# The second layer's mixer: input projection as seven half products, retention and mixing behind it

## The chip, the cores and the metric

One core of a Trainium2 chip. The metric is the device time of one execution in microseconds (us), the median of several runs; profiles show one execution, by engine: TensorE (PE, its weight loads PEld), VectorE (DVE), ScalarE (ACT), GpSimd (POOL) and SyncE's queue (SP), which issues every DMA here.

## The reference

Two layers over 1024 rows of width 1024, f32. Each layer computes x <- LN(alpha x + mixer(x)) and then x <- LN(alpha x + SwiGLU(x)), with 2816 hidden columns. The change concerns the mixer of layer 1 (the second):

```
hproj = x @ w_in_odd            # 1024 x 2560: q 256, k 256, v 512, gate 512, z-part 1024 (u 512, z 512)
o_c = group_norm_heads(retention(q, k, v)) * silu(gate)         # 4 heads
u, z = gelu(...);  z = layer_norm(z);  o_d = u * (tril(w_s) @ z + b_s)   # blocks of 128 rows, 4 groups
mix = concat([o_c, o_d]) @ w_out_odd
```

## The kernel before

Every f32 product is three passes of f32r matmuls (high x high, high x low, low x high). So each operand is split into a high and a low part: an ACT cast and a DVE subtraction (`split`, L64 to L67). Weights come from HBM through raw tiles (3 to 4) into weight units of 128 x 2 x 512 (a ring of 8, with more of them in the feed-forward stages).

Activations stand transposed in X tiles (128 features x 4 blocks of features x high, low x 512 rows). `row_to_x` (L144) makes 128 rows of one: four PE transposes into a PSUM bank, an ACT cast, and for the low part either a DVE subtraction or (pe=True) another matmul and ACT cast; then the bank is free.

The feed-forward stages (`rest`, L852) already use seven half products for a 2 x 2 block product (Winograd's form, in place of eight): the weights of a column pair are combined on DVE (`others`), seven operands are split and seven products of 12 matmuls run into PSUM banks, with sums between. The down product loops over half products i = 1, 5, 6, 3, 7, 2, 4; behind them come the row norms, and `transposed` makes X tiles for the next layer: the second half of the rows first for each block, the two transposing banks being taken in program order.

`odd_mixer` (L627) projects without that: `gemm_T` (L113) with 512 moving columns for q, k, gate and u (`proj_T`), `gemm_R` (L123) with 256 for v and z, 24 matmuls per output block over all 8 feature blocks. `gate()` makes z first, block of rows by block of rows. Then `weave` fills the gaps of retention's chains (scores, values, group norm, output) with projection steps: a main generator yields its cost, and so much of the fill times a rate is issued behind it. PE's order in the mixer is this written order (manual_schedule); the other engines are ordered by Tile's list scheduler, by priority and a simulated time.

`OutProj` (L193) takes finished 128-row pieces of the transposed mixer output (`take`: stored to o_rows in HBM, the last kept), reads them back and splits them (`split_o`), and multiplies in two halves of the contraction: `first` (pieces 0 to 3, retention's, 16 products of 12 matmuls with ALPHA x added) and `second` (pieces 4 to 7). `first` asks for the first rows of the other half itself if the kept piece is there; `middle` reads the rest.

## Time and profile before

| what | value |
|---|---|
| median of 3 runs | 2304.25 us (2302.89 to 2306.63) |
| profiled execution | 2303.7 us, span 2302.0 us, mean granted clock 0.995 |
| busy share of the span | PE 98%, PEld 82%, DVE 66%, ACT 40%, POOL 5% |
| the chain that ended last | PE 82%, DVE 8%, DMA 6%, ACT 2% |
| HBM | 218.64 MB read, 87.56 MB written |

The second layer's mixer runs from about 1256 us (first z matmul) to 1588 us (end of the first half of its output projection). PE records are pipelined and overlap: a group's mean is longer than the spacing of its matmuls, which is read from the chain (a stretch's time over its count).

### The profile page before, as it was taken

How to read it: one execution, taken by the hardware profiler on the slowest of the kernel's cores; microseconds unless marked ns; L12 is line 12 of the kernel's file. 1: busy time of each engine (PE TensorE's matmuls, PEld its weight loads, DVE VectorE, ACT ScalarE, POOL GpSimd, SP SyncE). 2: the span in 40 equal slices, each digit the busy share in tenths (PEclk: the TensorE clock that was granted, in tenths of full speed). 3: DMA queues.
4: the chain of work that ended last, by engine and by line, in shares of the span. 5: the costliest groups of instructions: out<-in, count | busy, mean ns of one | idle time of the engine just before them, and what ended most of it. 6: DMA issues, size and time to landing. Idle time of an engine off the chain costs nothing.

```text
span 2302.0 us, 30422 instructions
## 1 busy us (share of the span) xinstructions
PE 2258.9 (98%) x11380; PEld 1878.4 (82%) x11380; DVE 1512.4 (66%) x3030; ACT 918.0 (40%) x1756; POOL 124.5 (5%) x111
## 2 busy tenths in 40 slices
PE   8999999999999999999999999999999999999997
PEld 7888888878788888888887988888788888888885
DVE  4767676777877676756577423455967776656568
ACT  4545455553543333334443321122543333334432
POOL 0000000001200000000021100000300000000003
PEclk9999999999999999999999999999999999999998
DMA  5212121234255454558655111144345454558553
GB/s 170 69 47 59 42 58 37 67 98 132 79 178 188 147 169 141 174 194 290 200 184 180 47 47 42 47 130 158 126 140 169 147 182 134 178 182 294 187 179 136
DMA packets 195539, 312.37 MB, mean 136 GB/s; under 512 B 14784, under 2 KB 98368, under 8 KB 195392
## 3 DMA queue, kind: packets, MB, share of 16 engines
q1 hardware_dynamic: 195392, 310.44, 41.3%
q8 instruction: 89, 1.46, 0.2%
q14 instruction: 58, 0.48, 0.1%
HBM read 218.64 MB, written 87.56 MB: 133 GB/s over the span
## 4 chain that ended last, share of the span: by engine, by line
PE 82%; DVE 8%; DMA 6%; ACT 2%; issue 1%; POOL 0%; POOLq 0%; SPq 0%; ACTq 0%; DVEq 0%
PE pd L1110 9%; PE bx_g L875 8%; PE bx_u L875 8%; PE bw_u L875 5%; PE bw_g L875 5%; PE vps L127 4%; PE qps L117 4%; PE kps L117 3%; PE po_o L234 3%; PE bv_u L875 3%; PE bv_g L875 3%; PE bz_u L875 2%; PE bz_g L875 2%; DMA raw_d<-d_ops 2%; PE ovps L127 2%; PE zps L127 2%
## 5 line engine op out<-in xcount | busy, mean ns | idle before, releaser
L1110 PE MATMUL pd<-w_d,h 128*128 128x512 f32 x1716 | 393.3, 390 | 3.5 <-DVE w_d L67 2.1
L1110 PEld LDWEIGHTS pd<-w_d,h 128*128 128x128 f32 x1716 | 322.0, 188 | 72.8 <-DVE w_d L67 3.5
L875 PE MATMUL bx_g<-xs,w_g 128*128 128x512 f32 x792 | 192.2, 390 | 0.5 <-ACT w_g L66 0.5
L875 PE MATMUL bx_u<-xs,w_u 128*128 128x512 f32 x792 | 190.9, 389 | 0.0
L875 PEld LDWEIGHTS bx_g<-xs,w_g 128*128 128x128 f32 x792 | 148.2, 188 | 32.2 <-ACT w_g L66 0.8
L875 PEld LDWEIGHTS bx_u<-xs,w_u 128*128 128x128 f32 x792 | 148.6, 188 | 30.8
L67 DVE TENSOR_TENSOR w_d<-raw_d,w_d 128x512 fp32r<-128x512 f32 x149 | 97.7, 686 | 103.1 <-ACT w_d L66 102.9
L66 ACT CAST w_d<-raw_d 128x512 fp32r<-128x512 f32 x149 | 86.6, 618 | 152.9 <-DMA raw_d<-d_ops 88.9
L875 PE MATMUL bw_u<-xs,w_u 128*128 128x512 f32 x528 | 130.7, 389 | 0.0
L875 PE MATMUL bw_g<-xs,w_g 128*128 128x512 f32 x528 | 130.7, 389 | 0.0
L67 DVE TENSOR_TENSOR h<-raw_h,h 128x512 fp32r<-128x512 f32 x143 | 98.8, 715 | 33.4 <-ACT h L66 33.0
L440 ACT ACTIVATE s<-s,mx 128x640 f32<-128x640 f32 (+7 forms) x128 | 93.3, 731 | 65.6 <-DVE mx L438 65.3
L875 PEld LDWEIGHTS bw_u<-xs,w_u 128*128 128x128 f32 x528 | 99.0, 188 | 21.0 <-DVE cy L926 0.4
L127 PE MATMUL vps<-w_v,x 128*128 128x256 f32 x768 | 114.5, 293 | 1.5 <-DVE k L340 1.5
L875 PEld LDWEIGHTS bw_g<-xs,w_g 128*128 128x128 f32 x528 | 99.0, 188 | 20.5
L117 PE MATMUL qps<-x,w_q 128*128 128x512 f32 x384 | 110.0, 408 | 0.6 <-ACT w_q L66 0.5
L117 PE MATMUL kps<-x,w_k 128*128 128x512 f32 x384 | 110.5, 408 | 0.0
L66 ACT CAST h<-raw_h 128x512 fp32r<-128x512 f32 x143 | 83.8, 618 | 59.1 <-DMA raw_h<-h_ops 52.2
L127 PEld LDWEIGHTS vps<-w_v,x 128*128 128x128 f32 x768 | 100.8, 193 | 6.5 <-issue 4.6
L66 ACT CAST w_u<-raw_u 128x512 fp32r<-128x512 f32 x118 | 73.3, 623 | 77.8 <-issue 40.9
L67 DVE TENSOR_TENSOR w_u<-raw_u,w_u 128x512 fp32r<-128x512 f32 x118 | 80.8, 686 | 35.5 <-ACT w_u L66 35.4
L66 ACT CAST w_g<-raw_g 128x512 fp32r<-128x512 f32 x110 | 68.3, 625 | 88.2 <-PE bw_g L875 30.8
(591 smaller groups left out, 4184.9 us busy)
## 6 DMA issues: line engine op xcount, KB each, us to landing
raw_h<-h_ops SPq DMA_DIRECT2D x70, 512.0 KB, 4.2
h_ops<-cy SPq DMA_DIRECT2D x110, 256.0 KB, 3.3
raw_g<-in_ffn_w_gate_dram SPq DMA_DIRECT2D x44, 512.0 KB, 4.7
raw_u<-in_ffn_w_up_dram SPq DMA_DIRECT2D x44, 512.0 KB, 5.4
raw_dr<-in_ffn_w_down_dram SPq DMA_DIRECT2D x44, 512.0 KB, 3.6
d_ops<-raw_dr SPq DMA_DIRECT2D x44, 512.0 KB, 2.7
raw_d<-d_ops SPq DMA_DIRECT2D x40, 512.0 KB, 4.9
raw_d<-in_ffn_w_down_dram SPq DMA_DIRECT2D x30, 512.0 KB, 4.8
```

What stands on the lines that cost most here:

```text
L66: A.copy(dst[:, 0], src)
L67: V.tensor_sub(dst[:, 1], src, dst[:, 0].bitcast(F32))
L117: T.matmul(ps, w[k // 4][:, a, (k % 4) * P:(k % 4 + 1) * P], xh[k // 4][:, k % 4, b, :], start=n == 0, stop=n == 3 * KT - 1)
L127: T.matmul(ps, xh[k // 4][:, k % 4, a, b4 * P:(b4 + 1) * P], ws[k // 2][:, b, (k % 2) * 256:(k % 2) * 256 + 256], start=n == 0, stop=n == ...
L234: T.matmul(ps, self.xo[h][c][:, k, a, b4 * P:(b4 + 1) * P], self.w[c][2 * nh + k // 2][k % 2][:, b], start=n == 0, stop=n == 11)
L440: A.activation(s[:, :L], s[:, :L], AF.Exp, bias=self.mx[:, m:m + 1], scale=0.125, accum_out=self.sm[:, m:m + 1])
L875: T.matmul(ps, w[:, a, k * P:(k + 1) * P], X[i][:, k, b, :], start=first and n == 0, stop=n == 11, skip_group_check=more or not first)
L1110: T.matmul(bank[side][b4], hs[k][:, a, b4 * P:(b4 + 1) * P], ds[k][:, b], start=fresh and k == 0 and n == 0, stop=k == NP - 1 and n == 2, ...
```

## The change

The layer's input projection is done as seven half products over 512 x 512 blocks of x. v and z together are one such block product (`rows_product`: seven of 48 matmuls, 512 moving columns, k outside and the four row blocks inside). q, k, u and gate are six column pairs (`pair`: seven products of 12 matmuls). The combined weights for v and z are made in the first layer's gate and up loop (`row_ops`, rounds 0 to 3) and stored in z_ops. X1, X2, X3 and X7 come from the end of the first layer; X6, X4 and X5 from sums of the rows in place (`sums`), transposed between the products. u and gate go to HBM (gu_rows) and are read back; u, then gate, into one tile. Only then come retention and mixing: mixing woven into head pair 0's states, then both pairs' heads woven with `first`, whose half is now the mixing's (begin=4). y tiles, misc, qk and gu share one pool of two.

```diff
-        def __init__(self, dram, res, name):
+        def __init__(self, dram, res, name, begin=0):
...
         def take(self, k, h, o):
+            k = (k - self.begin) % KT
...
+    def row_weights(i, pick=None):
+        c, h = {1: (512, 0), 2: (512, 1), 4: (2048, 1)}.get(i, (0, 0))
+        r = []
+        for j in (0, 2):
+            if i in (1, 2, 4):
+                src = w_in_odd[0][(4 * h + j) * P:(4 * h + j + 2) * P, c:c + 512].rearrange("(k p) f -> p k f", p=P)
+            else:
+                src = z_ops[i in (3, 5), j:j + 2, :, slice(0, 512) if i in (6, 3) else slice(512, 1024)].rearrange("k p f -> p k f")
+            r += load_w(src, f"zw{i}_{j}", pick)
+        return r
...
+        op = OutProj(w_out_odd[0], res, "o", begin=4)
...
+                def rows_product(ps, i, ds, first=True):
+                    for k in range(4):
+                        for b4 in range(4):
+                            for n, (a, b) in enumerate(PASSES):
+                                T.matmul(ps[b4], X[i][:, k, a, b4 * P:(b4 + 1) * P], ds[k][:, b], start=first and k == 0 and n == 0,
+                                         stop=k == 3 and n == 2, skip_group_check=True)
+                def sums():
+                    for b4 in range(4):
+                        y0a, y0b, y1a, y1b = (y[h][:, b4, c * 512:(c + 1) * 512] for h in (0, 1) for c in (0, 1))
+                        V.tensor_sub(y1a, y1a, y0a)
+                        V.tensor_sub(y1b, y1b, y1a)
+                        V.tensor_sub(y0b, y1b, y0b)
+                    for i, h, c in ((6, 1, 1), (4, 0, 1), (5, 1, 0)):
+                        for b4 in range(4):
+                            row_to_x(y[h][:, b4, c * 512:(c + 1) * 512], X[i], b4, trp, f"o{i}{b4}")
+                z = banks(False, "p3")
+                rows_product(z, 3, zw)
...
+                f = banks(True, "p7")
+                rows_product(f, 7, row_weights(7))
...
+                rows_product(z, 1, row_weights(1))
...
+                sums()
+                f = banks(True, "p2")
+                rows_product(f, 2, row_weights(2))
...
+                rows_product(z, 6, row_weights(6), first=False)
...
+                rows_product(f, 4, row_weights(4))
+                misc = ypool.tile([P, 4, 1024], F32, tag="y", name="misc")
...
+                for b4 in range(4):
+                    V.tensor_sub(zv[:, b4], zv[:, b4], f[b4])
+                    z_rows(b4)
+                rows_product(z, 5, row_weights(5), first=False)
+                for b4 in range(4):
+                    V.tensor_add(v[:, 4 + b4], z[b4], v[:, 4 + b4])
+                    V.tensor_add(zv[:, 4 + b4], z[b4], zv[:, 4 + b4])
+                    z_rows(4 + b4)
...
+                qk = ypool.tile([P, 4, 1024], F32, tag="y", name="oqk")
+                pair(256, qk[:, 2:4], "ok")
+                pair(0, qk[:, 0:2], "oq")
+                for n, (c0, func) in enumerate(((1536, AF.Gelu_apprx_tanh), (1792, AF.Gelu_apprx_tanh),
+                                                (1024, AF.Silu), (1280, AF.Silu))):
+                    c = pair(c0, misc[:, 0:2], f"gu{n}")
+                    for i in (0, 3, 2, 1):
+                        A.activation(c[i], c[i], func)
+                        S.dma_start(gu_rows[n][:, i // 2, (i % 2) * 512:(i % 2 + 1) * 512], c[i])
...
+            gu = ypool.tile([P, 4, 1024], F32, tag="y", name="gu")
+            for n in (0, 1):
+                S.dma_start(gu[:, 2 * n:2 * n + 2], gu_rows[n])
...
+            def mixing():
+                yield from ws_transposed()
+                for g in range(4):
+                    yield from mixed(g)
+                for n in (0, 1):
+                    S.dma_start(gu[:, 2 * n:2 * n + 2], gu_rows[2 + n])
             r0, r1 = Retention(0), Retention(1)
-            weave([], [gate()], 0)
-            weave([ws_transposed()], [r0.qkv()], 1.0)
-            weave([r0.heads()], [r0.gates(), r1.qkv()], 3.6)
-            weave([r1.heads()], [r1.gates(), mix(0), mix(1)], 2.4)
             first = op.first()
-            for g in range(4):
-                weave([mixed(g)], [mix(g + 2)] if g < 2 else [first] if g == 3 else [], 5.0)
+            weave([r0.states()], [mixing()], 3.0)
+            weave([r0.heads()], [first], 1.3, rest=False)
+            weave([r1.states(), r1.heads()], [first], 1.7)
             op.middle()
...
+            def row_ops(j):
+                r = [raw_tile(f"zr_{j}_{i}") for i in (0, 1)]
+                for i in (0, 1):
+                    for z, c in ((0, 512), (1, 2048)):
+                        S.dma_start(r[i][:, z * 512:(z + 1) * 512], w_in_odd[0][(4 * i + j) * P:(4 * i + j + 1) * P, c:c + 512])
...
+                        if not last and p < 4:
+                            row_ops(p)
...
+                    if h:
+                        row_to_x(yb, xn[3], b4, trp, nm + "c", pe=True)
+                        t3 = raw_tile(f"t3_{nm}")[:, :512]
+                        G.tensor_sub(t3, yb, ya)
+                        row_to_x(t3, xn[7], b4, trp, nm + "g", pe=True)
+                    else:
+                        row_to_x(ya, xn[1], b4, trp, nm + "a")
+                        row_to_x(yb, xn[2], b4, trp, nm + "b")
```

## Rows read from the trace of the kernel before

**Rows 1.** Busy time by stage: window, length, PE, PEld, DVE, ACT, POOL, clock, DMA.

```profile
640.00:1033.00 393.00, 393.00 (x1735) 325.05 (x1733) 273.28 (x433) 147.71 (x259) 0.00 (x0) 1.00 0.51 170
1257.00:1310.00 53.00, 51.35 (x420) 50.10 (x419) 26.76 (x52) 22.24 (x47) 7.64 (x8) 1.00 0.24 68
...
1356.00:1447.00 91.00, 91.00 (x519) 77.09 (x518) 34.18 (x97) 15.84 (x30) 4.05 (x4) 1.00 0.15 47
```

**Rows 2.** The chain of waits, 1180 to 1700: start, length in us, engine, tile, line.

```profile
1275.04 35.76 PE zps L127 x298
1310.80 0.44 PE wsps L663 x4
1311.23 10.92 PE oq0ps L117 x48
...
1370.35 1.08 PE rs L750 x8
...
1515.39 0.89 PE mix L813 x8
...
1654.86 2.73 PE bx_u L875 x12
```

**Rows 3.** Busy time of the z product alone at the entry (PE, PEld, ACT).

```profile
1256.10:1269.00 12.90, 9.27 (x66) 8.45 (x67) 0.73 (x2) 1.00 0.68 189
```

**Rows 4.** Timeline at the entry: start, length, engine, line, operation.

```profile
1268.16 0.60 PE L148 MATMUL xt_f<-ident,yf 128*128 128x128 f32 x4
...
1268.80 0.59 ACT L151 CAST xn<-xt_f 128x512 fp32r<-128x512 f32 x1 [1.29 <-PE xt_f L148]
1269.42 0.69 DVE L156 TENSOR_TENSOR xn<-xt_f,xn 128x512 fp32r<-128x512 f32 x1 [1.18 <-ACT xn L151]
...
1271.87 1.08 ACT L154 CAST xn<-xt_f 128x512 fp32r<-128x512 f32 x2
```

**Rows 5.** Groups by line, 1033 to 1350: the norm of z on DVE.

```profile
L182 DVE SCALAR_TENSOR_TENSOR zv<-zv,rstd_sgu,gb_sgu 128x512 f32<-128x512 f32 x8 | 6.0, 751 | 3.1 <-POOL rstd_sgu L169 3.1
L181 DVE SCALAR_TENSOR_TENSOR zv<-zv,mv_sgu,gb_sgu 128x512 f32<-128x512 f32 x8 | 5.9, 743 | 0.0
L164 DVE BATCH_NORM_STATS2 st_sgu<-zv 128x6 f32<-128x512 f32 x8 | 5.5, 693 | 1.7 <-ACT zv L677 1.7
```

**Rows 6.** DMA issues of the whole run: count, KB each, median us to landing.

```profile
raw_h<-h_ops SPq DMA_DIRECT2D x70, 512.0 KB, 4.2
h_ops<-cy SPq DMA_DIRECT2D x110, 256.0 KB, 3.3
...
raw_h<-h_ops SPq DMA_DIRECT2D x14, 256.0 KB, 3.7
...
o_rows_o<-oTr SPq DMA_DIRECT2D x8, 256.0 KB, 2.0
...
o_rows_o<-oTm SPq DMA_DIRECT2D x6, 256.0 KB, 4.1
```

**Rows 7.** Groups by line, 1355 to 1600: ACT and DVE operations of mixing and output.

```profile
L66 ACT CAST xo_o<-raw_o_o 128x1024 fp32r<-128x1024 f32 x6 | 6.3, 1050 | 21.0 <-PE po_o L234 10.2 <-DMA raw_o_o<-o_rows_o 8.2 <-PE u3ps L117 2.6
...
L815 DVE TENSOR_TENSOR mixs<-mix,bsb 128x512 f32<-128x512 f32 x8 | 5.4, 687 | 9.9 <-PE mix L813 9.9
...
L717 ACT ACTIVATE og<-og00ps 128x512 f32<-128x512 f32 x2 | 1.2, 599 | 9.8 <-PE og00ps L117 9.8
```

**Rows 8.** The chain of waits, 1352 to 1372: one state update of retention.

```profile
1359.72 0.43 PE kv L735 x2
```

**Rows 9.** Timeline at the end of the first half of the output projection.

```profile
1549.07 47.26 PE L234 MATMUL po_o<-w_o,xo_o 128*128 128x512 f32 x207
...
1588.22 0.37 SPq L88 DMA_DIRECT2D raw_o_o<-o_rows_o  x1
...
1592.92 1.57 ACT L66 CAST xo_o<-raw_o_o 128x1024 fp32r<-128x1024 f32 x2 [3.52 <-DMA raw_o_o<-o_rows_o]
```

**Rows 10.** Busy time in the burst of row norms at the end of the run.

```profile
2260.00:2270.00 10.00, 4.29 (x15) 2.61 (x14) 10.00 (x7) 0.70 (x2) 6.59 (x3) 0.81 0.39 141
2270.00:2280.00 10.00, 10.00 (x39) 8.06 (x39) 9.45 (x21) 0.00 (x0) 1.46 (x1) 0.85 0.11 44
```

More of the change, by code (lines that the diff above doesn't have):

```diff
@@ L273, in second, with product, kf, operand @@
                 yield 0.65
+    def product(ps, w, x, first=True, more=False):
+        n = 0
+        for k in range(4):
+            for a, b in PASSES:
+                T.matmul(ps, w[:, a, k * P:(k + 1) * P], x[:, k, b, :], start=first and n == 0,
+                         stop=n == 11, skip_group_check=more or not first)
+                n += 1
+    def kf(t):
+        return t.rearrange("p (k f) -> p k f", k=4)
+    def operand(src, i, nm):
+        u = w_unit(f"{nm}_{i}")
+        split(u.rearrange("p z (k f) -> p z k f", k=4), src)
+        return u
+    def row_weights(i, pick=None):
[8 more added lines that the diff above has]
+        return r
     def even_mixer():
@@ L649, in odd_mixer @@
[L649 removed]
+            bsb = p1.tile([P, 4, P], F32, name="bsb")
             S.dma_start(bsb, sgu_b[0].partition_broadcast(P))
@@ L790, in heads @@
                     self.sT, self.orow = {}, {}
-                    yield from self.states()
                     self.oT = [op_.tile([P, SEQ], F32, tag="oT", name=f"oTr_{self.p}{z}") for z in (0, 1)]
@@ L802, in heads @@
                             yield 1.0
-            def mix(g):
-                uT = uTs[g] = p2.tile([P, SEQ], F32, tag="uT", name=f"uT_{g}")
-                yield from proj_T(1536 + g * P, f"u{g}", lambda ps, sl: A.activation(uT[:, sl], ps, AF.Gelu_apprx_tanh))
             def mixed(g):
@@ L868, in rest @@
             X = [None] * 8
-            def product(ps, w, i, first=True, more=False):
-                n = 0
-                for k in range(4):
-                    for a, b in PASSES:
-                        T.matmul(ps, w[:, a, k * P:(k + 1) * P], X[i][:, k, b, :], start=first and n == 0,
-                                 stop=n == 11, skip_group_check=more or not first)
-                        n += 1
-            def kf(t):
-                return t.rearrange("p (k f) -> p k f", k=4)
-            def operand(src, i, nm):
-                u = w_unit(f"{nm}_{i}")
-                split(u.rearrange("p z (k f) -> p z k f", k=4), src)
-                return u
             def start(dram, p, nm):
@@ L894, in first_two @@
                 bx = accp.tile([P, 512], F32, tag="acc", name=f"bx_{nm}")
-                product(bx, m[2], 1, more=True)
+                product(bx, m[2], X[1], more=True)
                 bz = mm_tile(f"bz_{nm}")
-                product(bz, m[3], 2)
+                product(bz, m[3], X[2])
                 return bx, bz
@@ L1040, in transposed @@
                 def transposed(h, b4):
-                    for c in (0, 1) if not last else ():
-                        row_to_x(y[h][:, b4, c * 512:(c + 1) * 512], xn[h][c], b4, trp, f"f{layer}{h}{b4}{c}", pe=h == 1)
+                    if last:
+                        return
+                    ya, yb = y[h][:, b4, ca], y[h][:, b4, cb]
+                    nm = f"f{layer}{h}{b4}"
+                    if h:
[6 more added lines that the diff above has]
+                        row_to_x(yb, xn[2], b4, trp, nm + "b")
                 def sum_up(i, b4, ps):
```

177 lines of the change are left out of this document (104 added, 73 removed).

## The prediction, made before the change was run

> **What bounds the kernel now.** I read the page's shares first: TensorE (PE) is busy 98% of the span, so only work taken off it, or waits put on it, can move the end. Then the stages [rows 1]: the first layer's gate and up stage, and the second layer's projections with retention show PE busy for their whole length; the entry to the second layer loses 1.65 us of 53. DVE is at 70% in the gate and up stage and at 38% in the retention stage, with room. Then the chain of waits, for the real price of a matmul: the records overlap, so I take a stretch of the chain and divide by its count. A moving operand of 512 columns costs 10.92/48 = 0.2275 us in the old projections and 2.73/12 = 0.2275 in a seven-product stage; 256 columns cost 35.76/298 = 0.120 [rows 2].
>
> **Matmuls removed and added.** Before, query, key, gate and u take 12 column blocks x 48 = 576 matmuls of 512 columns, 131.0 us; value and z take 2 x 384 = 768 of 256 columns, 92.2 us; together 223.2. After, six pairs of 84 and seven row products of 48 make 840 of 512 columns: 191.1. Twelve more groups of four transposes, for X6, X4 and X5, take 0.44 each [rows 2], 5.3. PE's own work falls by 223.2 - 191.1 - 5.3 = **26.8 us**.
>
> The Trainium skill, page "TensorE: Matmul & The Clock Gate", section "Back-to-back issue gap", gives N/2.4 GHz + 2.5 ns between issues at full clock: 0.216 us for 512 and 0.109 for 256 columns, which would save 576 x 0.216 + 768 x 0.109 - 840 x 0.216 = 26.7 us before the transposes, not 32.1, and the sum below would end 5.4 us later. Here the trace differs, most for the narrow ones (0.120), and I keep the rows.
>
> Everything else is about what PE waits for.
>
> **Entry.** The old first projection went row block by row block and needed only the finished block; it did 66 matmuls between 1256.1 and 1269 [rows 3], while the last blocks were still being transposed. The new p3 goes over k outside and all four blocks inside, so it stands until the last block of X3 is in. That block comes late because the transposes take turns in two PSUM banks in program order: one bank is held from the transposes (1268.16) over the ACT cast (1268.80) to the end of the DVE subtraction (1269.42 + 0.69), and the last block of the second half has its low part only at 1271.87 + 1.08 [rows 4]. Without ACT's copies and its table load for the old product I put X3 at 1269. Until then p3 can issue 9 matmuls, 2.0 us, where the old one had 66 x 0.12 = 7.9: **+6** (4 if the banks turn faster, 7.5 at 1272).
>
> **The sums.** PE's order here is written by hand: p1, then all 12 transpose groups, then p2. Two banks, 1.95 us each from transposes to release and some 0.15 to the next start [rows 4]: 6 x 2.1 = 12.6 us, of which 5.3 is work counted above: **+7.3**. If only DVE set the pace, 12 x 0.69 + 1.3 less 5.3 = 4.3; with four weight splits of p6 (0.69 each) between them, 10. The subtractions on y before them lie under p7 and p1 (22 us).
>
> **Row norms.** Behind p4 and p5 DVE gets 12 evacuations of 0.69 and eight row norms, each statistics 0.69 and two passes of about 0.75 [rows 5], 25.8 us in all, while PE has p5 (10.9) and two pair products (5.5) before it needs operand 6, for which DVE must also make three combinations and a split (2.8). 28.6 - 16.4 = 12, less what was done ahead in the 2 us before p4's end and what finds gaps while a norm waits for POOL's power: **+3**, from 0 to 9. Six pairs follow, each with 19.1 us on PE and some 10.5 on DVE; the gate and up stage runs the same mix with no PE wait [rows 1], so no charge.
>
> **The last phase.** E is the end of the last pair. The misc tile holds that pair's results, and the gu tile takes its slot, so the reload of u waits for: addition 0.69, Silu 0.6, store of 256 KB 3.3, read of 1 MB. For that size there is no row; 512 KB takes 4.2 and 256 KB 3.7 [rows 6], so 5.2 by their step, 8.4 as two reads in line. I take 5.2, as the queue is quiet there. u is there at E + 9.8. The Trainium skill, page "DMA: Bandwidth & Descriptors", section "Bandwidth", has 6.15 us for 1 MB, which would add 1 us to the sum.
> DVE then goes through 12 operations of 0.69 (bias and product of each mixing half) to the first half of the last group: E + 18.1. The row is stored (between 2.0 and 4.1, I take 3.0), read back (4.2) and cast (1.05) [rows 6, 7]: the third block of the first output product can run at E + 26.3. By the hand-written order PE has until there: states 2 x 0.44 + 7 x 0.43, transposing the mixing weights 0.44, eight mixing halves of 0.89, two score groups of 1.08 and six output matmuls [rows 2, 8]: 3.9 + 0.4 + 7.1 + 2.2 + 1.4 = 15.0. **+11.3.** All of head 0's values, later scores and output stand behind this product on PE. Low end, the shortest rows everywhere (both stores 2.0, the big read 4.2): 8; high end, the double read, 14 state updates and four weight splits between, a 4.1 store: 23. The constant tables (decay, mask, biases) are loaded at E - 2.7, when X5's memory comes free; SP issues them ahead of the gu reads, and they land under this wait. The gates' own reload follows the mixing and has over 20 us.
>
> **The tail.** Walking the weave's costs by hand, the place in the first half of the output projection that asks for the first rows of its other half now passes before head 3's first half is taken; so both reads of retention rows fall behind the first half, where before only one did. Before, the first half ended at 1549.07 + 171 x 0.2275 = 1588.0 (192 matmuls, 21 of them earlier), such a read was issued at 1588.22 and cast from 1592.92 [rows 9]; the next product then waited for nothing, as its half had been there. After, it waits for that cast, 1592.92 + 1.05 - 1588 = 6, less two transposes of 0.44: **+5** (0 if the read is issued earlier, 8 with the second cast).
>
> **First layer.** Four times in the gate and up stage come four reads of 256 KB, four DVE operations (2.7 us in a round of 38) and two stores; the cover is DVE's 30% and the lookahead of the raw tiles: **+0.5** (0 to 3). Four POOL subtractions at its end lie under the last product. Twenty-four more SP issues of some 0.35 us are spread over 150 us.
>
> **Clock.** Where PE was busy 4.3 of 10 us, the granted clock was 0.81 on the mean, and 0.85 in the next 10 us with PE full [rows 10], a mean of the full level (2.4 GHz) and the lower one (1.2): 1.5 us lost after one such wait. The last phase has one of that kind, the entry and the sums milder ones: **+2.5** (0 to 6).
>
> **Sum:** -26.8 + 6 + 7.3 + 3 + 11.3 + 5 + 0.5 + 2.5 = +8.8. The profiled execution took 2303.7 (span 2302.0 and 1.7 around it), 0.55 under the median of the runs, so nothing is shifted: **2312 us**. All low ends together give -26.8 + 16.3 = -10.5, all high ends some +40.
>
> **Rivals.**
> Forecast, 0.42: the waits as summed, 2303 to 2324.
> Last phase not held, 0.32: the mixing rows are back before PE needs them, because the list scheduler puts reload, mixing and store ahead of all else on SP and DVE. It decides from the point where the third output block can run at E + 15 in place of E + 26. Then 11.3 and 1.5 of clock go: 2299, between 2288 and 2306. For it: DMA moves only 47 to 68 GB/s in the old retention stage and DVE is a third busy. Against it: the chain store, read, 12 operations, store, read is serial whatever the order.
> DVE becomes the bound behind p4, 0.16: with strict program priority operand 6 waits for all eight norms, some 9 us more, and the last phase lies at its upper half: 2324, up to 2335. For it: DVE full and PE at 4.3 of 10 in a burst of norms [rows 10]; against it: those rows are twice as wide.
> The saving is smaller than counted, 0.10: the new products run above their 0.2275 for want of operands, since the pairs have 8 weight units and 3 raw tiles where the gate and up stage has 12 and 4. A quarter of the 26.8 missing gives 2319. Against it: PE there needs one operand in 2.7 us, and ACT and DVE make one in 0.7.
>
> **Numbers.** 0.2% (4.6 us) is about what can be told from no change. Faster: 0.03 + 0.18 + 0 + 0.01 = 0.22; within: 0.05 + 0.12 + 0 + 0.03 = 0.20; slower: 0.58. The range runs from the better part of the second case to most of the third, 2291 to 2332; the forecast's own range is 2303 to 2324.
>
> **What would show it.** Entry: PE with few p3 matmuls and a wait for ACT on X3. Sums: 48 transposes spread over about 12 us. Row norms: a PE wait for DVE on the first key pair's sixth operand. Last phase: some 11 us in which PE waits for the cast of the output's first operand, behind a read of gu rows. Tail: a PE wait of 5 us behind the read of retention rows. The prediction is wrong if the last phase shows PE full, or if the stage from p3 to the last pair is longer than about 76 + 115 + 5 + 17 us.

## The result, and the profile after

The changed kernel takes 2337.69 us (median of 4, 2334.34 to 2339.92) against 2303.57 (2301.43 to 2306.63) for the kernel before: ratio 1.0152, 95% interval 1.014 to 1.0164, so 34 us slower. Slower was forecast, but at 2312 and no more than 2332. The page of the changed kernel, with its span, PE's busy time and the granted clock:

```profile
span 2337.4 us, 29811 instructions
...
PE 2255.4 (96%) x10924; PEld 1851.0 (79%) x10924; DVE 1597.2 (68%) x3168; ACT 943.5 (40%) x1790; POOL 131.2 (6%) x115
...
PEclk9999999999999999999999999989999999999999
```

PE has 456 matmuls fewer than before (11380), yet its busy time fell by 3.5 us only, and it stands idle for 82 us in place of 43. Its mean clock went from 0.995 to 0.986. So of the 35.4 us between the two spans 39 are idle time, and the matmuls, which had 26.8 us less to do, took some 23 us longer than counted. An estimate from the mean clocks puts most of that down to the lower clock: (1 - clock) x span is 32.7 us after and 11.5 before.

**Where the time is lost.** The lag of the new kernel behind the old at marks that both traces have:

| mark | before | after | lag |
|---|---|---|---|
| first down product, layer 0 | 1033.90 | 1039.97 | 6.1 |
| first matmul of the second mixer | 1256.18 | 1268.57 | 12.4 |
| end of the output projection's first half | 1588.0 | 1622.5 | 34.5 |
| first down product, layer 1 | 2072.62 | 2116.64 | 44.0 |
| end of the span | 2302.0 | 2337.4 | 35.4 |

Stages of the changed kernel (columns as in [rows 1]); the first row answers to the first of [rows 1], where PE was busy throughout:

```profile
640.00:1033.00 393.00, 387.75 (x1707) 319.73 (x1706) 278.14 (x443) 140.23 (x249) 0.00 (x0) 1.00 0.56 187
...
1320.00:1340.00 20.00, 19.19 (x79) 15.57 (x80) 8.73 (x14) 5.31 (x10) 0.00 (x0) 0.83 0.17 54
1360.00:1380.00 20.00, 17.39 (x71) 13.94 (x70) 20.00 (x41) 7.56 (x13) 4.70 (x4) 0.91 0.17 53
...
1500.00:1520.00 20.00, 17.21 (x96) 14.78 (x96) 14.12 (x30) 1.63 (x2) 0.64 (x1) 0.79 0.64 231
1520.00:1540.00 20.00, 10.91 (x34) 7.47 (x34) 7.78 (x10) 3.13 (x3) 0.00 (x0) 0.64 0.76 266
1540.00:1560.00 20.00, 20.00 (x92) 15.21 (x92) 10.63 (x39) 0.00 (x0) 2.03 (x2) 0.93 0.13 42
1620.00:1640.00 20.00, 13.09 (x47) 9.42 (x46) 16.49 (x34) 6.34 (x9) 1.01 (x1) 0.87 0.74 235
```

What PE waited for from 1265 to 1700 us (us in total, times, longest):

```profile
PE po_o L237 <- ACT xo_o L66: 11.5, 3, 8.0
PE wsps L815 <- POOL wsr L808: 5.3, 1, 5.3
PE xt_o L148 <- DVE xn L156: 4.5, 5, 1.6
PE po_o L237 <- DVE ym L275: 3.7, 1, 3.7
PE bw_gu L284 <- DVE misc L768: 3.1, 4, 0.8
PE bx_ok L284 <- DVE zv L739: 2.6, 1, 2.6
```

Each is a place of its own: last phase and tail, last phase, sums, tail, pairs, norms. The sums and a pair on PE, as timeline:

```profile
1311.50 1.03 PE L148 MATMUL xt_o<-ident,yf 128*128 128x128 f32 x8
1314.18 1.25 PE L148 MATMUL xt_o<-ident,yf 128*128 128x128 f32 x8 [1.65 <-DVE xn L156]
...
1324.24 6.13 PE L687 MATMUL p<-w_zw,xn 128*128 128x512 f32 x19
...
1407.61 2.88 PE L284 MATMUL bw_oq<-xn,w_oq 128*128 128x512 f32 x12
1411.27 3.06 PE L284 MATMUL bw_oq<-xn,w_oq 128*128 128x512 f32 x12 [0.78 <-DVE oqk L768]
```

The transposes go two by two as the banks come free and take 1324.24 - 1311.50 = 12.7 us with 5.3 of work in them. In a pair the seventh product adds to the bank that the sixth has just filled; DVE must read it first (L768), and as PE's order is written by hand nothing else stands between: 0.78 us, six times over. The last phase on PE, then the same stretch on SP's queue:

```profile
1494.79 0.60 PE L841 MATMUL krps<-ident,oqk 128*128 128x128 f32 x4
1500.73 1.12 PE L815 MATMUL wsps<-ident,wsr 128*128 128x128 f32 x4 [5.34 <-POOL wsr L808]
...
1531.33 3.34 PE L237 MATMUL po_o<-w_o,xo_o 128*128 128x512 f32 x6 [8.03 <-ACT xo_o L66]
```

```profile
1514.33 0.42 SPq L951 DMA_DIRECT2D gu<-gu_rows  x1
1515.15 7.99 SPq L207 DMA_DIRECT2D o_rows_o<-oTm  x4
1523.18 0.43 SPq L951 DMA_DIRECT2D gu<-gu_rows  x1
1523.72 1.79 SPq L88 DMA_DIRECT2D raw_o_o<-o_rows_o  x3
```

With E = 1494.8 the end of the last pair, the third output block runs at E + 36.5, in place of the E + 26.3 of the forecast. And behind the first half, the tail:

```profile
1622.49 1.84 PE L896 MATMUL rt<-ident,orow 128*128 128x128 f32 x8
1627.53 7.40 PE L237 MATMUL po_o<-w_o,xo_o 128*128 128x512 f32 x24 [3.20 <-ACT xo_o L66]
1638.59 12.57 PE L237 MATMUL po_o<-w_o,xo_o 128*128 128x512 f32 x48 [3.65 <-DVE ym L275]
```

24 matmuls of 512 columns took 7.40 us here, 0.31 each in place of 0.2275. In the first layer the profile has PE waits that were not there before, and one of DVE (640 to 1045, DVE to 800):

```profile
PE bw_g L284 <- DVE cy L1020: 3.9, 2, 3.0
PE bw_u L284 <- DVE cy L1020: 1.3, 1, 1.3
```

```profile
DVE zr L1043 <- DMA zr<-in_w_in_odd_dram: 14.8, 4, 5.4
```

DVE stands 3.7 us a round, and runs nothing meanwhile, in front of row_ops' first combination, whose reads have not landed. The additions of the products (cy, L1020), for which PE waits, stand behind it in DVE's queue.

### The profile page after: what moved, and what is told of

Its sections match the earlier page's. It is cut to its first block, busy times and chain, and to the rows that moved or that the text cites. A ratio compares the mean times of both kernels' runs of the same rounds, so it can differ in the third digit from the quotient of the medians.

```text
span 2337.4 us, 29811 instructions
## 1 busy us (share of the span) xinstructions
PE 2255.4 (96%) x10924; PEld 1851.0 (79%) x10924; DVE 1597.2 (68%) x3168; ACT 943.5 (40%) x1790; POOL 131.2 (6%) x115
## 4 chain that ended last, share of the span: by engine, by line
PE 82%; DVE 10%; DMA 4%; ACT 2%; issue 2%; POOL 0%; SPq 0%; POOLq 0%; DVEq 0%; ACTq 0%
PE pd L1231 16%; PE bx_u L284 7%; PE bx_g L284 7%; PE bw_g L284 4%; PE bw_u L284 4%; PE vps L127 4%; PE qps L117 4%; PE po_o L237 4%; PE kps L117 3%; PE p L687 3%; PE bv_u L284 2%; PE bz_g L284 2%; PE bz_u L284 2%; PE bv_g L284 2%; PE po_e L237 2%; PE pv L521 2%
## 5 line engine op out<-in xcount | busy, mean ns | idle before, releaser
L237 PE MATMUL po_o<-w_o,xo_o 128*128 128x512 f32 x384 | 106.0, 420 | 16.6 <-ACT xo_o L66 11.5
L237 PEld LDWEIGHTS po_o<-w_o,xo_o 128*128 128x128 f32 x384 | 73.2, 198 | 35.0 <-ACT xo_o L66 12.1
```

Source lines behind the costliest of these rows:

```text
L237: T.matmul(ps, self.xo[h][c][:, k, a, b4 * P:(b4 + 1) * P], self.w[c][2 * nh + k // 2][k % 2][:, b], start=n == 0, stop=n == 11)
```

## The experiments

Marks of single profiled executions scatter by some 2 us, and medians of four runs by about as much (the single runs of one version lie up to 18 us apart), so segments between two marks of one trace are read beside the times. The versions were timed in groups, each beside the kernel before, which took 2302.2 to 2305.0 in them; a ratio is to the kernel before in the same group. "The pairs" is from the first key product to E, "behind E" from E to the first down product of layer 1 (621.9 us in the changed kernel).

**row_ops on POOL, and without row_ops.** In row_ops the four `V.tensor_...` become `G.tensor_...`:

```diff
-                V.tensor_add(wb1, wb0, wb1)
+                G.tensor_add(wb1, wb0, wb1)
```

> The four combinations of each round of row_ops run on POOL instead of DVE; loads and stores stay as they are. Theory (queue order): in the changed kernel DVE stands 14.8 us in four rounds in front of these combinations, waiting for its own reads (3.7 us a round), and the first layer's products wait for DVE behind it. POOL has nothing to do in that stage, so its wait holds nobody up: the first down product moves from 1039.97 back to about 1034.5, and the whole run to 2327 to 2333 us (5.5 to 11 less). Rival (the reads and stores themselves compete with the weight loads): the products go on waiting, now for reads, the first down product stays within 1.5 us of 1040, and the time within 2 us of 2337.7.

> row_ops is left out altogether, and the second layer reads plain weights of the same size in place of the four combined ones, so it leaves out the combinations of v's and z's weights. Theory (queue order): the same as with POOL within 1.5 us at the first down product (1033.9 before the change, so 1034 to 1035.5). Rival (transfers compete): this run alone returns the 6 us, so it lies 5 us or more below the run with POOL.

```diff
-                        if not last and p < 4:
-                            row_ops(p)
```

With POOL the PE waits of this stage fall to 0.7 us and the first down product comes at 1034.89; that execution took 2331.25, but the median of its four runs is 2339.45 (2331.25 to 2346.54), so the times do not show the gain. Without row_ops (the combined weights are left out) the mark is 1032.35 and the median 2331.27 (2323.18 to 2334.13). By the mark of the run with POOL DVE's wait is the larger part, as in the theory; but the mark without row_ops lies 2.5 us further (1.5 was allowed) and the median 8.2 us lower, which is what the rival named. So the reads and stores, or POOL itself, keep a part. POOL is no free engine: its rows, then DVE's, in one round:

```profile
710.64 1.73 POOL L1044 TENSOR_TENSOR zr<-zr 128x512 f32<-128x512 f32 x1
```

```profile
710.53 0.69 DVE L1003 TENSOR_TENSOR s_g<-raw_g,raw_g 128x512 f32<-128x512 f32 x1 [3.25 <-DMA raw_g<-in_ffn_w_gate_dram]
711.17 1.75 DVE L67 TENSOR_TENSOR w_g<-raw_g,w_g 128x512 fp32r<-128x512 f32 x1
```

While POOL combines, DVE's split of 128 x 512 takes 1.75 us in place of 0.68, and POOL's own operation 1.73, where the one before it, with DVE idle, took 1.28. Over all runs the first down product stands at 1041.0 on the mean of the ten with row_ops as in the change (1038.88 to 1043.68), at 1036.4 with POOL (three), at 1032.35 and 1036.11 without, and before at 1033.90. The stretch behind it, to the first matmul of the second mixer, is shorter without row_ops too: 223.5 and 223.8 us, for 228.2 to 231.2 in nine of those ten (the tenth has the edit of the norms below) and 222.3 before. Why was not tried.

**The pairs' order.**

```diff
-                    bv = mm_tile(f"bv_{nm}")
-                    product(bv, o4, X[4])
...
                     product(bw, o5, X[5], more=True)
+                    product(bx, o7, X[7], first=False)
...
+                    product(bv, o4, X[4])
```

> In the six column pairs the fourth and fifth operands' products change places: 1, 2, 6, 5, 7, 4, 3, so that product 4 runs between the two that share bank bw. Theory: the wait of 0.78 to 0.85 us before the last product of each pair goes (bank bw is read by DVE right before it is added to), the pair's period falls from 20.16 to 19.1 us, the end of the last pair comes 6 to 6.6 us earlier, and the run takes 2331 to 2332 us. Rival (the pair's operands set the period, through three raw tiles and eight weight units): the wait only moves to another product of the pair, the period stays at 20 and the time within 2 us of 2337.7.

The pairs took 115.9 us in place of 122.6: 6.7 fewer, for the 6 to 6.6 expected. What PE still waited for in them:

```profile
PE bx_ok L284 <- DVE zv L739: 2.6, 1, 2.6
PE bw_ok L284 <- DVE oqk L766: 1.2, 1, 1.2
```

The median, 2336.39, is only 1.3 lower, not the 6 of the theory; in the profiled execution the first layer was 3.7 us later than in the changed kernel's. The segment decides for the theory on the wait; why the other runs gained so little in time is not shown.

**The mixing weights' read first.** Tile, read and mask move up together.

```diff
+            wsr = p2.tile([P, 4, P], F32, tag="tmp", name="wsr")
+            S.dma_start(wsr, sgu_w[0].rearrange("g t s -> t g s"))
...
             gu = ypool.tile([P, 4, 1024], F32, tag="y", name="gu")
```

> Only the order of issue: the mixing weights' read goes ahead of the u reload and the six constant tables, so that their mask is done some 4 us earlier. Theory (what stands behind the wait on PE counts): PE no longer waits 5.3 us at the transposes of the mixing weights, so the state updates run while u is on its way, DVE's 12 mixing operations are no longer spread over 13.6 us by state updates, and the third block of the output product comes 4 to 5 us earlier: 2332 to 2334 us. Rival (u's reload, which lands 10.7 us after the last pair, sets the phase whatever stands before it): the wait at the transposes goes to the mixing products, the third block stays within 1.5 us of 36.5 us behind the end of the last pair, and the time within 1.5 us of 2337.7.

The wait at wsps is gone and the third block comes at E + 33.6: 2.9 us of the 4 to 5, and 1.7 behind E; the time is 2338.02. Neither theory as stated: the wait covered some state updates, but u sets the larger part.

**The gates' reload behind the rows' reads.** The reload leaves `mixing` and is called in `first`.

```diff
                 self.split_o(0, h)
+            if behind:
+                behind()
```

> Only the order of issue: the gates' reload (two reads of 1 MB) goes behind the first four reads of output rows instead of before them. In the changed kernel the third block of the output product starts 36.5 us after the last pair's end; its read is issued behind the second of these reloads and lands 6.5 us later, beside both. Theory (SP's order and the shared transfer): the read comes 0.5 to 1 us earlier and takes 4 to 4.5 us, so the third block starts at 32.5 to 34 us behind the last pair's end, 2.5 to 4 us earlier, and the end of the output projection's first half follows by as much. Rival (the gates then come too late): PE gains that at the third block and loses it where head 0's rows are multiplied with their gate; the end of the first half stays within 1 us.

The third block is at E + 36.1 and the time 2340.67: nothing gained. SP's rows tell why:

```profile
1526.37 0.43 SPq L956 DMA_DIRECT2D gu<-gu_rows  x1
1526.92 1.73 SPq L88 DMA_DIRECT2D raw_o_o<-o_rows_o  x3
```

SP's order is as before. Only PE's order is the written one here; the list scheduler put the issue that could go first in front. So this run tells nothing about either theory, and a later one makes the reload wait by its memory.

**u in place.**

```diff
-                for n, (c0, func) in enumerate(((1536, AF.Gelu_apprx_tanh), (1792, AF.Gelu_apprx_tanh),
-                                                (1024, AF.Silu), (1280, AF.Silu))):
-                    c = pair(c0, misc[:, 0:2], f"gu{n}")
+                for n, (c0, func) in enumerate(((1024, AF.Silu), (1280, AF.Silu),
+                                                (1792, AF.Gelu_apprx_tanh), (1536, AF.Gelu_apprx_tanh))):
+                    c = pair(c0, misc[:, 2:4] if n == 2 else misc[:, 0:2], f"gu{n}")
...
-            gu = ypool.tile([P, 4, 1024], F32, tag="y", name="gu")
+            gu = misc
```

> The gates' two pairs come before u's, u's results stay in the tile in which they are made (no store, no reload), and the mixing weights' read goes first. Nothing of u is left to wait for: the mixing can begin some 3 us after the last pair's end in place of 10.7. Theory (the way of u over HBM is the first link of the chain): the first product of mixing and u comes 7 us earlier, the third output block at 28 to 30 us behind the last pair's end in place of 36.5, and the end of the first half 6.5 to 8.5 us earlier, with up to 1.5 us more from the clock. Rival (the rows' own way over HBM and DVE's row of operations set the phase): mixing starts earlier but is drawn out by state updates, and the third block comes less than 4 us earlier (the run with the weights' read alone gained 2.9).

```profile
1526.49 3.34 PE L237 MATMUL po_o<-w_o,xo_o 128*128 128x512 f32 x6 [7.64 <-ACT xo_o L66]
```

E is 1496.10 here, so the third block comes at E + 30.4, 6.1 us earlier, and behind E 612.4 us pass, 9.4 fewer. That is near the theory's 28 to 30 and past the rival's 4. The way of u is the first link; 7.64 us of the last one stay. The median, 2335.79 (2331.15 to 2341.71), is only 1.9 lower.

**The weave's rates.**

```diff
-            weave([r0.heads()], [first], 1.3, rest=False)
-            weave([r1.states(), r1.heads()], [first], 1.7)
+            weave([r0.heads()], [first], 1.0, rest=False)
+            weave([r1.states(), r1.heads()], [first], 1.5)
```

> Only two rates of the weave: 1.0 and 1.5 in place of 1.3 and 1.7, so that head 3's first half is taken before the place that asks for the first rows of the other half. Theory (the tail's waits are the read that is issued too late): the waits behind the end of the first half (3.2 and 3.7 us in the changed kernel, and the half clock behind them) go, 6 to 9 us between the end of the first half and the first down product of the second layer, less 0 to 2 us for thinner cover in the heads: 2329 to 2333 us. Rival (DVE's evacuations and norms set the tail): the wait for DVE at the second half stays at 3 us or more, and less than 3 us are gained.

```profile
1624.52 15.49 PE L237 MATMUL po_o<-w_o,xo_o 128*128 128x512 f32 x60
1640.44 11.18 PE L237 MATMUL po_o<-w_o,xo_o 128*128 128x512 f32 x48 [0.43 <-DVE ym L275]
```

Both waits of the tail are gone but for 0.43 us; behind E 615.7 us pass, 6.1 fewer. Of that the thinner cover had taken back its part (PE waits 4.3 us for rows of heads, 1.2 before). The median is 2336.54, above the 2329 to 2333 expected.

**The transposes between p1's steps.** `sums` yields behind each group, and p1's product takes one group ahead of each step from the fifth.

```diff
                         for b4 in range(4):
+                            if fill and 4 * k + b4 > 3:
+                                next(fill, None)
```

> The twelve groups of transposes for X6, X4 and X5 stand between the steps of p1 on PE, from its fifth step on, in place of behind it. Theory (the two transposing banks set a pace of about 1 us a group, while PE has only 0.44 of work in it): p1's other 10 us cover that pace, the 12.7 us behind p1 shrink to 0 to 2 while p1 grows by the 5.3 us of transposes, and the end of the last pair comes 6 to 7.5 us earlier: 2330 to 2332 us. Rival (DVE, which makes the low parts and p2's splits and has the row subtractions ahead of them, sets the pace): p1 stretches to 20 us or more, and less than 3 us are gained.

```profile
1304.73 0.60 PE L148 MATMUL xt_o<-ident,yf 128*128 128x128 f32 x4
1305.08 0.94 PE L689 MATMUL p<-w_zw,xn 128*128 128x512 f32 x3
...
1317.53 12.75 PE L689 MATMUL p<-w_zw,xn 128*128 128x512 f32 x55
```

A group every 1.13 us and no wait: from the first down product to the first key product 323.5 us pass in place of 332.2, 8.7 fewer (the wait of 7.4 and the low clock behind it). The median is 2333.2 us, 4.5 lower; 2330 to 2332 was expected.

**Gates apart, on top of u in place.**

```diff
+            gt0 = p1.tile([P, 2, SEQ], F32, name="gt0")
+            S.dma_start(gt0, gu_rows[0])
...
+            for z in (0, 1):
+                S.dma_start(qk[:, 2 * z], gu_rows[1][:, z])
             weave([r1.states(), r1.heads()], [first], 1.7)
```

> On top of the run that keeps u in place and reads the mixing weights first: the gates of head pair 0 are read into a tile of their own as soon as the projections' memory is free, those of pair 1 into the places of pair 0's query and key once these have been used. So no gate reload of 1 MB stands on SP, or in the transfers, ahead of the output rows' reads. In the run without this the third output block started 30.4 us behind the last pair's end, with the read issued 2.05 us after the second reload and landing beside it. Theory (the reload ahead of the read): 26 to 28 us, and 2 to 4 us less at the end of the first half: 2331 to 2334 us. Rival (the rows' own store, three reads of 512 KB and cast take that time whatever runs beside them): less than 1 us gained at the third block, the time within 1.5 us of 2335.8.

The third block comes at E + 28.2, 2.2 us earlier, just past the theory's upper bound. But 612.2 us pass behind E as in the run without: the wait for DVE in the tail grew from 4.1 to 6.5. The median is 2333.55 us, within the theory's range.

**Together.** The edits above as named in each expectation.

> The changed order of the pairs' products, u in place with the mixing weights' read first, the two lower weave rates and the transposes between p1's steps, together; row_ops stays on DVE. Theory (these are separate waits on PE's path): their gains, read as the segments of their single runs (6.7, 9.4, 6.1 and 8.7 us), add to 31, less some for clock that each gave back alone: 2306 to 2311 us. Rival (they share a cause, or the time comes back later as the next wait): less than 22 us gained, 2316 us or more.

> The same with row_ops' combinations on POOL. Theory (DVE's wait for its own reads): 5 to 8 us less than the run with the combinations on DVE, 2299 to 2305 us, about the kernel before. Rival (POOL's move helped only in the one profiled execution; its other runs did not show it): within 2.5 us of the run with DVE.

> The same with POOL, and with the gates read apart. Theory: 2 to 4 us less than the run before it, 2295 to 2302 us, which would be under the kernel before (2303). Rival (the rows' own way sets it): within 1.5 us of the run before it.

The first takes 2315.46 (2311.69 to 2320.84): 22.2 of the 31 us, between the theory and the rival. In its profile the pairs gave 6.6, the stretch up to them 7.2 of 8.7, and the stretch behind E 12.7 of 15.5. The single edits had lowered the medians by 1.3, 1.9, 1.2 and 4.5 only, 8.9 together: each alone shows less in the time than in its segment. With POOL it is 2312.93 (ratio 1.0038, 1.0024 to 1.0051), 2.5 less, so no more than the rival allows. With the gates apart it is 2307.76 (ratio 1.0021, 1.0008 to 1.0034), 5 less; the theory had 2 to 4 less, but a time under 2302, and the two intervals overlap.

> The run with all edits and the gates apart, but with row_ops left out, so that the second layer reads plain weights in place of the combined ones (it leaves out the combinations of v's and z's weights, as the earlier run without them did). It bounds what the four rounds of row_ops cost, on POOL or on DVE. Theory (they cost the first layer 4 to 6 us by single profiled executions): the first down product from 1037.95 back to 1032 to 1033, and the time from 2307.8 to 2299 to 2303 us, under or at the kernel before. Rival (the first layer's loss is jitter of the reads): within 2.5 us of 2307.8.

2303.45 us (ratio 0.9999, 0.9989 to 1.0008), 4.3 less: row_ops' cost in the mended kernel, even on POOL. The first down product came at 1036.11, not at 1032 to 1033; the first mixer matmul came 10.4 us earlier than in the traced execution with row_ops.

```diff
-                r = [raw_tile(f"zr_{j}_{i}") for i in (0, 1)]
+                r = [zrp.tile([P, 1024], F32, tag=f"zr{i}", name=f"zr_{j}_{i}") for i in (0, 1)]
```

> The run with all edits and the gates apart, with row_ops back on DVE, but reading into two tiles of its own, with the reads issued at the start of the round and the combinations at its end; two of the first layer's 12 weight units pay for the memory. Theory (DVE's wait for its own reads is the cost): the wait of DVE at row_ops goes from 3.7 us a round to under 0.5, the first down product starts at 1033 to 1035.5, and the time is 2301 to 2305 us. Rival (four more reads and two stores a round, or the shorter ring of weight units, cost as much): the first down product at 1037 or later, time within 2 us of 2307.8 or above.

DVE's wait for these reads fell to 1.3 us in all, but it now waits longer for the gate weights (17.0 us), and the first down product was at 1039.98 here and at 1035.67 and 1036.06 in the two runs that follow with the same gate and up stage. 2308.91 us (2299.80 to 2318.05). Mark and time of this run are the rival's, the two later marks lie between theory and rival: not settled. Where the wait was taken from the combinations, part of it went to the other reads.

```diff
                 pair(256, qk[:, 2:4], "ok")
+                for t in range(4):
+                    z_rows(t)
                 pair(0, qk[:, 0:2], "oq")
...
+                        if i == 5 and self.p:
+                            yield 2.0
```

> On top of the run with own tiles: the eight norms of z go behind the first and the second column pair (four each), and the last output rows of head 3 get six more steps of output products ahead of them. Theory: the wait of 2.6 us for DVE at the first pair's sixth operand goes, and so do most of the 4.3 us in which the transposes of head rows wait for DVE: 4 to 6 us less than the run with own tiles. Rival (DVE owes the same work within the next 20 us, so that the waits move to the second pair's operands): less than 1.5 us.

2305.62 us (ratio 1.0011, 1.0003 to 1.002), 3.3 less than the run with own tiles (1.0024, 1.001 to 1.0038), between theory and rival; the intervals overlap. The longest waits that PE still has in the mixer, of 20.5 us in all (5.4 before):

```profile
PE bx_ok L284 <- DVE zv L740: 2.6, 1, 2.6
PE po_o L237 <- DVE xo_o L67: 2.6, 1, 2.6
PE rt L901 <- DVE orow L893: 2.5, 1, 2.5
PE mix L930 <- DVE sts L858: 1.9, 2, 1.0
PE kv L855 <- DVE kr L848: 1.4, 1, 1.4
```

The wait at the first pair stays at 2.6 us without the norms ahead of it, so the norms were not its cause. It stands before the first matmul of the key pair, and who ends it is the addition into zv (L740), which reads a bank of p5: the pair's first bank comes from the same four, and DVE has two additions to make from each. The gain is in the transposes of head rows (4.3 to 2.5 us; behind E 604.3 us pass for 608.1) and in the first layer, which scatters.

**The last addition of the norms.**

```diff
-            G.tensor_add(row, row, gb[1])
+            V.tensor_add(row, row, gb[1])
```

(only for the row norms at the end of the first layer's down product.)

> On top of that: in the row norms at the end of the first layer's down product the last step, an addition over 128 x 1024, goes from POOL to DVE. In the changed kernel DVE's splits of 128 x 512 took 2.88 us and 3.50 for two while POOL was at these additions (1208 to 1223), where they take 0.68 alone, and PE waits 2.7 us (6.2 in the run with all edits) for such a split behind them. Theory (the two engines hinder each other): the splits go back to 0.7, DVE is done earlier although it has four operations of some 1.2 us more, the PE wait falls under 1.5 us, and the time by 2 to 5 us. Rival (DVE is simply full there): the wait grows by 2 us or more.

PE's longest waits in that down product (1045 to 1260 us) in the kernel before, then in the changed kernel, both for weight splits; then POOL's and DVE's rows of the kernel without this edit, and DVE's with it:

```profile
PE pd L1110 <- DVE w_d L67: 2.1, 4, 0.8
```

```profile
PE pd L1231 <- DVE w_d L67: 5.0, 6, 2.7
```

```profile
1207.69 9.45 POOL L179 TENSOR_TENSOR yf<-yf,gb_ffn 128x1024 f32<-128x1024 f32 x3 [1.76 <-DVE yf L178]
```

```profile
1206.40 5.69 DVE L178 TENSOR_TENSOR yf<-yf,gb_ffn 128x1024 f32<-128x1024 f32 x3
1212.01 2.88 DVE L67 TENSOR_TENSOR w_zw<-raw_zw,w_zw 128x512 fp32r<-128x512 f32 x1
```

```profile
1202.29 1.28 DVE L67 TENSOR_TENSOR h<-raw_h,h 128x512 fp32r<-128x512 f32 x2
1203.49 1.22 DVE L179 TENSOR_TENSOR yf<-yf,gb_ffn 128x1024 f32<-128x1024 f32 x1
```

A split that takes 0.68 alone took 2.88 while POOL was adding. On DVE the addition takes 1.22, PE waits no more for splits at that place, and the time is 2295.69 (2293.93 to 2300.03), ratio 0.997 (0.9959 to 0.9981): the first version that is faster than the kernel before, and the gain is twice what was expected of this edit. The edit also takes POOL's 2.7 to 3.2 us a row out of the way of the rows, so how much of the gain is the hindrance and how much the shorter way, these runs do not tell.

> The changed kernel as it is, with only the last step of the row norms at the end of the first layer's down product on DVE in place of POOL. Theory (what was 10 us in the run with all edits is this step's own cost, and it stands in the changed kernel too, which the prediction did not see): the PE waits for weight splits there (5.0 and 1.1 us in all) and the lower clock behind them go, the first mixer matmul comes 7 to 10 us earlier, and the time is 2328 to 2331 us. Rival (it only pays once the other waits are gone): less than 4 us.

> The kernel before, with the same step on DVE. It tells how much of that step's cost is the change's. The kernel before has seven waits of 0.23 to 0.83 us for weight splits at that place, 3.5 us in all, and a granted clock of 0.93 and 0.90 in the two stretches around them. If the cost is as old as the kernel before: 2298 to 2301 us (3 to 5 less), and then the changed kernel has lost 2.5 us or more on top at this place. If it is the change's alone: within 1.5 us of 2303.2.

The changed kernel with this edit alone takes 2331.38 (6.3 less; ratio 1.012 for 1.0152, which is 7.4); the kernel before with it takes 2296.28 (2294.05 to 2298.01), ratio 0.9963 (0.995 to 0.9976). So the edit is about as good for either: its 8 us were lost before the change too, and of the version that beats the kernel before, nothing is the change's. From the first down product to the first mixer matmul the edit leaves 218.5 us of 228.6 in the changed kernel and 215.4 of 222.3 in the kernel before: of the 6.3 us that the change lost in this stretch, half is gone with it and 3.1 stay. The mended change and the kernel before are not told apart with the edit (2295.7 and 2296.3; ratios 0.997 and 0.9963, the intervals overlap), and some 2.4 us apart without (2305.6, 2303.2).

## Why the prediction was wrong, step by step

| step | forecast | measured |
|---|---|---|
| PE's own work | -26.8 | holds: a pair without its wait is 115.9 / 6 = 19.3 us, 84 x 0.2275 = 19.1 |
| first layer, gate and up | +0.5 | +6.1 |
| end of the first layer's down product | 0 | +6.3 |
| entry | +6 | +2.1 |
| sums | +7.3 | +7.4 |
| row norms | +3 | +2.6 |
| pairs | 0 | +6.3 |
| last phase | +11.3 | +21.5 |
| tail | +5 | +9.6 |
| clock (mixer) | +2.5 | +9.2 |
| end of the run | 0 | -8.6 |

The measured column adds to 35.7, against 35.4 between the spans. The entry is PE's idle time from 1260 to 1280 us in the changed kernel (3.8) less the 1.65 of [rows 1]. The last phase is 36.5 less the 15.0 of work that the prediction counted into it; the clock term is (1 - granted clock) x PE's busy time in the windows behind the sums and the norms (3.3 and 1.6) and what the matmuls behind the third block took over their full price (4.3); the other steps hold their own slow matmuls. Of the 27 us between the sum of 8.8 and the measured 35.7 the last phase has 10.2, the clock 6.7, the pairs and the end of the first layer's down product 6.3 each, the gate and up stage 5.6 and the tail 4.6; the entry and the end of the run give 12.5 back.

A stage from p3 to the last pair longer than some 213 us was named as a sign of being wrong. It took 226.2 (1268.57 to 1494.79).

**The step that failed** is twice the same one: an operation was costed by its busy time on an engine with room, where its place in a queue decides. "The cover is DVE's 30%" for row_ops took no account of DVE standing in front of reads that had not landed: 3.7 us a round, 14.8 in all, of which the products' slack covered more than half (PE waited 5.2, and the stage ended 6.1 later). "The gate and up stage runs the same mix with no PE wait, so no charge" for the pairs took the list scheduler's order for granted: there the other product's matmuls stand between a bank's read and its next addition, here the written order has nothing. The run with the changed order shows the second (6.7 us). For the first, the mark came 5 to 9 us earlier without row_ops, and some 4 earlier, on the mean of three, both with POOL and with tiles of its own, where DVE no longer stood there; so DVE's place in front of the reads is more than half of it, and what the rest is stays open. The 6.3 us at the end of that layer's down product had no term at all: half of them go with the norms' addition on DVE, and the rest stays open as well.

**The last phase** had the right mechanism, and its size was off by 10 us. It is the largest single miss. u was ready at E + 10.7, for E + 9.8: its last store was issued at E + 1.7 and took 4.0 us to land, where 3.3 were counted, and the read that DVE waited for, issued behind it, took 4.9. The four reads of this size between 1490 and 1530 us took 4.9 to 7.0, with this median:

```profile
gu<-gu_rows SPq DMA_DIRECT2D x4, 1024.0 KB, 6.1
```

The prediction took 5.2 by the step from 256 to 512 KB. The Trainium skill, page "DMA: Bandwidth & Descriptors", section "Bandwidth", has 6.15 us for a load of this size that GpSimd issues. The median here, on SP's queue, agrees, but the read that set u's time was faster. From u to the last group's first half the forecast had 12 operations of DVE, 8.3 us; it took from 1505.5 to 1519.1, with state updates between them, which had waited behind the mask of the mixing weights (with that mask earlier the third block gained 2.9 us). Then the row's store was queued on SP with the last group's second half behind it, and its read was issued behind the gates' reload, at 1523.72, and needed 6.5 us to land beside that transfer in place of 4.2. "The gates' own reload has over 20 us" asked when the gates were needed, not what stood behind them.

**The tail** was the mechanism foreseen from [rows 9] (the run with other rates returned 6.1 us); the second wait, for DVE, and the lower clock over the first 24 matmuls are what it lacked. **Sums** came as summed from [rows 4]. **Row norms** came out right in size for a wrong reason: the wait is for a bank of p5 ahead of the first product, not for operand 6 behind the norms; with the norms moved away it stayed. **The entry** was overpaid: by the trace p3 had done 11 of its matmuls by the time X3's last low part was there (1279.9), near the 9 allowed, but that was 11.3 us behind its first matmul, in place of 12.8, and PE spent much of it on transposes.

**Clock.** One long wait and two milder ones were counted for 2.5 us, and the granted clock fell behind four places: 0.79 and 0.64 around the last phase, 0.87 in the tail, 0.83 behind the sums, 0.91 behind the norms.

**The end of the run** gave 8.6 us back, and no step spoke of it: the kernel before waits 5.8 us for DVE in the last down product, beside [rows 10], with the lower clock; in the changed kernel, whose down product there was not edited, no such wait stands. The kernel before keeps its tail from the same mark when its norms' addition is moved (229.5 us), while all versions of the change have some 221 to 223.5. So these 8.6 us are luck, and without them the miss would be larger. Which of the scheduler's choices does it was not tried.

**The rivals.** "Last phase not held" is refuted, DVE behind p4 too (2.6 us). "The saving is smaller than counted" fell as put, since neither units nor raw tiles were short; but the pairs did run above their price, for the bank.

**What stays of the 26.8.** With the waits that were found mended, about nothing. The traced execution of the version at 2305.6 (span 2300.8, 1.2 under the kernel before) has 15.1 us more of waits in the mixer than the kernel before, some 9 more of clock deficit by the same windows (0.67 from 1500 to 1520), and comes 1.8 us later to the first down product and 4.6 more to the first mixer matmul; the end of the run gives 6 back. With the 26.8 that is -2 us, close to the spans' -1.2.

## What to carry to other kernels

Cost a new operation by what its queue stands in front of, not by its engine's busy share: here DVE's 14.8 us in front of late reads came back as 5.2 us of waits on PE. Where an order is written out by hand, look for each result bank that is read and then added to, and put an independent product between. When a projection is taken out from under retention, what it covered must be counted as well as what it cost: here 26.8 us of matmuls went, and 39 us of idle time and some 23 of slower matmuls came; with the waits mended, still about as much as went.

## What the runs showed of the hardware

- POOL and DVE hinder each other on elementwise work in SBUF: a DVE split of 128 x 512 takes 0.68 us alone, 1.75 beside POOL's subtraction of 128 x 512, and 2.88 beside its addition of 128 x 1024 with a broadcast constant; POOL's subtraction takes 1.28 with DVE idle and up to 1.73 beside it. Taking four such additions from POOL gained 8.7 us in the kernel before.
- The order in which transfers are issued is the scheduler's even where PE's is written out: putting the gates' reload behind the rows' reads in the program left SP's order as it was, since those reads had to wait for a store. The mixing weights' read, which waits for none, did come first when it was moved up.
- Behind waits of 2.6 to 8 us matmuls ran at the lower of the two levels (1.2 GHz) for a while: six of 512 columns in 3.34 us at 1531.33, over twice the price at the full one. So a wait in this kernel cost about half as much again as its own length: 4.3 us behind the one of 8.0, 1.6 behind the one of 2.6.
